# A two-block kernel on one core: the order of transposes, filling products and low parts in the second block's attention

## The chip, the cores and the metric

One core of a Trainium2 chip runs the whole program. The metric is device time in microseconds, the median of several runs. Work goes to in-order queues: TensorE (PE, with its weight loads as PEld), VectorE (DVE), ScalarE (ACT), GpSimd (POOL), and SyncE (SP), which issues most loads.

## The reference, cut to what matters

Two transformer blocks over 256 rows of 1024 columns, in fp32. The first holds two attentions and a mixture of 64 experts. The second holds a mixer and, in its second layer, the attention that the change touches: 16 query heads of 64 columns, 4 key heads, 256 context keys and a window over 256 latent keys, a sink logit for each head.

```
def window_attention(q, k, v, k_ctx, v_ctx, sink):
    ...
        s_win = jnp.einsum('bqkgd,bjkd->bkgqj', qb, kb).astype(jnp.float32) * scale
        s_win = jnp.where(valid, s_win, NEG_INF)
        s_ctx = jnp.einsum('bqkgd,bjkd->bkgqj', qb, k_ctx).astype(jnp.float32) * scale
        p = sink_softmax(jnp.concatenate([s_ctx, s_win], axis=-1), sink_b)
        vals = jnp.concatenate([v_ctx, vb], axis=1)
        return jnp.einsum('bkgqj,bjkd->bqkgd', p.astype(v.dtype), vals)
...
            q, k, v, g = split_c(h @ w_in)
            o = window_attention(q, k, v, k_c, v_c, sink_logit[i])
            y = (o * jax.nn.silu(g)) @ w_out_c[i]
            x = x + gate * y
    return rms_norm_2(x, final_g)
```

## The kernel before, in words

Each engine runs its instructions in the order in which the program emits them. Large products are made from high and low parts: a weight tile is cast to a rounded type on ScalarE (line 129, the high part), VectorE subtracts that from the original (line 130, the low part), and three matmuls (high x high and the two mixed ones) stand in for a product of full precision. Both parts of one unit lie in a tile `hl`, of which there are three.

The class `Dense` holds a queue of such products. Each of its entries has a `prep` (a load of 1 MB for every second unit, then cast and low part, through `hl_unit`) and a `run` (the matmuls, and after the last of a block its evacuation). `step()` fills the queue up to two entries ahead, takes the first, fills again, and runs the entry it took. So a unit is prepared two steps before its products.

The second block's attention is a loop of 19 turns. In turn `n`:

- `w_a(n)`: scores of two heads for one of two query halves into two PSUM banks (two bf16 matmuls add the mask); VectorE takes their maxima (line 2018), joins the sink (2021, 2023); ScalarE takes exponentials with their sums (2027, 2028)
- `w_b(n-1)`: VectorE adds and inverts the sums and scales one head's weights (2033 to 2035), ScalarE the other's (2036)
- `w_d((n-6)/2)`, in even turns from 6 on: weighted sums over values (`ps_o`), gated by VectorE (2061) and split into `hab`, the left operand of the last products (cast 129 on ScalarE, 130 on VectorE)
- `D.step(steps[n])`: the products that fill TensorE: the second half of the queries (turns 0, 1, 3, 4; the rotary position code is applied at turn 4's end, lines 1910 to 1914), the gates (`ps_dt`, with tanh and a product at lines 1932 and 1933 after every second unit), and from turn 13 on the output projection
- `heads(n-2)`, in turns 6 to 9: transposes of two more heads' queries, evacuated by ScalarE and VectorE (1992, 1993)
- `w_t(n-3)`: eight transposes of the weights of turn n-3 into two PSUM banks of a pool of two (`ps_pt`, line 2046), copied out by ScalarE (2051) and VectorE (2049) for `w_d`

`steps` is written out by hand: 2, 1, 0, 1, 1, 1, 0, 0, 2, 1, 1, 0, 1, 1, 0, 1, 0, 1, 0. After the loop come `w_d(7)`, the last products, their residual and the final norm.

Of the kernel before, what the change touches and what calls it, by code (L numbers as in the profile page):

```python
# [10 lines left out]
F = mybir.dt.float32  # L11
# [4 lines left out]
OP = mybir.AluOpType  # L16
# [16 lines left out]
def kernel(ctx: ExitStack, tc: tile.TileContext, A, out, dbg=None):  # L33
    nc = tc.nc
    V, S, G, T = nc.vector, nc.scalar, nc.gpsimd, nc.tensor
# [15 lines left out]
    def bank(shape, name="ps", pool=None):  # L51
        n = 1
        for s in shape[1:]:
            n *= s
        t = (pool or psum).tile([128, 512], F, name=name, tag="ps")
        v = t[:shape[0], :n]
        if len(shape) == 3:
            v = v.rearrange("p (a b) -> p a b", b=shape[2])
        elif len(shape) == 4:
            v = v.rearrange("p (a b c) -> p a b c", b=shape[2], c=shape[3])  # L60
        return v

    def mm(o, l, r, start, stop):
        T.matmul(o, l, r, start=start, stop=stop)  # L64

    def mm3(o, l, r, start, stop):
        mm(o, l[0], r[0], start, False)
        mm(o, l[0], r[1], False, False)
        mm(o, l[1], r[0], False, stop)

    def kp(w2):
        return w2.rearrange("(k p) n -> p k n", p=128)
# [13 lines left out]
    def hl_tile():  # L86
        line.append(line.pop(0))
        return hlp[line[-1]].tile([128, 2, 1024], R, name="hl", tag="hl")

    def load(view, dims):  # L90
        t = raw_tile()
        n = 1
        for d in dims:
            n *= d
        v = t[:, :n]
        if len(dims) == 2:
            v = v.rearrange("p (k n) -> p k n", n=dims[1])
        nc.sync.dma_start(v, view)
        return v
# [28 lines left out]
    def split(hi, lo, src):  # L128
        S.copy(hi, src)  # L129
        V.tensor_tensor(lo, src, hi.bitcast(F), OP.subtract)  # L130

    def hl_unit(raw, pool=None):

        k, n = raw.shape[1], raw.shape[2]
        t = (pool.tile([128, 2, 1024], R, name="hl", tag="hl") if pool else hl_tile())[:, :, :k * n].rearrange("p h (k n) -> p h k n", n=n)
        split(t[:, 0], t[:, 1], raw)
        return t[:, 0], t[:, 1]


# [4 lines left out]
    class Dense:  # L144


        def __init__(self, bufs=3, ahead=2):
            self.bufs, self.ahead, self.live = bufs, ahead, 0
            self.todo, self.ready = [], []

        def nat(self, act, w3, c0, w, evac, plan=None):
            nk = w3.shape[1]
            plan = plan or PLAIN[:nk // 2]
            job = {}

            def prep(q):
                u, s = q // 2, q % 2
                if s == 0:
                    job["raw"] = load(w3[:, 4 * u:4 * u + 4, c0:c0 + w], (4, w))
                job[q] = hl_unit(job["raw"][:, 2 * s:2 * s + 2])  # L160

            def run(parts):
                if "ps" not in job:
                    job["ps"] = [bank([128, 512], "ps_d") for _ in range(2)]
                done = []
                for q, t in parts:
                    hl = job[q]
                    for k in range(2):
                        kk = 2 * q + k
                        mm3(job["ps"][t][:, :w], [a[:, kk, 128 * t:128 * t + 128] for a in act],  # L170
                            (hl[0][:, k], hl[1][:, k]), kk == 0, kk == nk - 1)
                    if q == nk // 2 - 1:
                        done.append(t)
                    if (q, t) == max((x for st in plan for x in st if x[0] == q), key=lambda x: order_of[x]):
                        self.live -= 1
                        del job[q]
                for t in done:
                    evac(t, c0, w, job["ps"][t][:, :w])

            order_of = {x: i for i, x in enumerate(x for st in plan for x in st)}  # L180
            seen = set()
            for parts in plan:
                new = [q for q, _ in parts if q not in seen]
                seen.update(new)
                q = new[0] if new else None
                self.todo.append((q is not None and (lambda q=q: prep(q)), lambda parts=parts: run(parts)))

        def tr(self, act, w3, c0, evac):
            job = {}

            def prep(cb):
                if cb == 0:
                    job["raw"] = load(w3[:, :, c0:c0 + 256], (8, 256))
                job[cb] = hl_unit(job["raw"][:, :, 128 * cb:128 * cb + 128])

            def run(cb):
                if cb == 0:
                    job["ps"] = bank([128, 2, 256], "ps_dt")
                hl = job.pop(cb)
                self.live -= 1  # L200
                for k in range(8):
                    mm3(job["ps"][:, cb], (hl[0][:, k], hl[1][:, k]), (act[0][:, k], act[1][:, k]), k == 0, k == 7)
                if cb == 1:
                    evac(c0, job["ps"])

            for cb in range(2):
                self.todo.append((lambda cb=cb: prep(cb), lambda cb=cb: run(cb)))
# [12 lines left out]
        def step(self, n=1):  # L220
            for _ in range(n):
                self.fill(self.ahead)
                if not self.ready:
                    return
                run = self.ready.pop(0)
                self.fill(self.ahead)
                run()

# [303 lines left out]
    def mixer(D, hook, pool, wk, hT, head):  # L532
# [57 lines left out]
        vg = pool.tile([128, 4], F, name="vg")  # L590
        nc.gpsimd.dma_start(vg, A["v_norm_g_2"].rearrange("o (h c) -> c (o h)", c=128))
        step(4)
        V.tensor_scalar(st_v[:, 0, 0:2], st_v[:, 0, 0:2], 1.0 / 512, None, op0=OP.mult)
        for t in range(2):
# [54 lines left out]
    def residual(wk, x, gate, then=None):  # L649

        def f(t, c0, w, ps):
            tmp = wk.tile([128, 512], F, name="tmp")
            V.tensor_tensor(tmp, ps, gate[:, c0:c0 + w], OP.mult)
            V.tensor_tensor(x[:, t, c0:c0 + w], x[:, t, c0:c0 + w], tmp, OP.add)
            if then:
                then(t)
        return f
# [5 lines left out]
    D = Dense()  # L663
# [558 lines left out]
    D = Dense()  # L1222
# [613 lines left out]
    D, hook, hT = Dense(), {}, []  # L1836
# [24 lines left out]
    with ExitStack() as st:  # L1861
# [4 lines left out]
        with ExitStack() as s2:  # L1866
# [31 lines left out]
            later = gate_later(mx, gb)  # L1898
            D, mx2 = mixer(D, hook, mx, wk, hT, head)
# [131 lines left out]
        def w_b(n):  # L2031
            p, sm, es = wst[n]
            V.tensor_add(sm, sm, es)
            V.reciprocal(sm, sm)
            V.tensor_scalar(p[:, 0], p[:, 0], sm[:, 0:1], None, op0=OP.mult)
            S.activation(p[:, 1], p[:, 1], AF.Copy, scale=sm[:, 1:2])

        def w_t(n):
            c, t = wunits[n]
            p = wst.pop(n)[0]  # L2040
            if t == 0:
                wpt[c] = ring.tile([128, 2048], F, name="w", tag="w").rearrange("p (j k n) -> p j k n", j=2, k=4)
            for j in range(2):
                ps = bank([128, 4, 128], "ps_pt", psbg)
                for kt in range(4):
                    T.transpose(ps[:, kt], p[:, j, 128 * kt:128 * kt + 128], ident)
                o = wpt[c][:, j, :, 128 * t:128 * t + 128]
                if j:
                    V.tensor_copy(o, ps)
                else:  # L2050
                    S.copy(o, ps)

        def w_d(c):
            ps = bank([128, 256], "ps_o")
            pt = wpt.pop(c)
            g = 64 * (c // 2)
            for kt in range(4):
                for j in range(2):
                    mm(ps[64 * j:64 * j + 64], vcat[:, kt, g:g + 64], pt[:, j, kt], kt == 0, kt == 3)
            t1 = wk.tile([128, 256], F, name="t1")  # L2060
            V.scalar_tensor_tensor(t1, ps, 0.5, sg[:, c], op0=OP.mult, op1=OP.mult)
            split(oT[0][:, c], oT[1][:, c], t1)
# [13 lines left out]
        steps = (2, 1, 0, 1, 1, 1, 0, 0, 2, 1, 1, 0, 1, 1, 0, 1, 0, 1, 0)  # L2076
        w_oc = kp(A["w_out_c_2"][0])
        D.nat(oT, w_oc, 0, 512, residual(wk, X, gb))
        for n in range(19):
            if n < 16:  # L2080
                w_a(n)
            if 1 <= n < 17:
                w_b(n - 1)
            if n >= 6 and n % 2 == 0:
                w_d((n - 6) // 2)
            D.step(steps[n])
            if 6 <= n < 10:
                heads(n - 2)
            if 3 <= n:
                w_t(n - 3)  # L2090
        w_d(7)
        fg = load(A["final_g_2"].rearrange("(o d) -> o d", o=1).to_broadcast([128, 1024]), (1024,))
        o = ring.tile([128, 2048], F, name="w", tag="w").rearrange("p (t n) -> p t n", t=2)
# [97 lines left out]
```

## Time and profile before

| | |
|---|---|
| median of 3 runs | 1149.74 us (1148.93 to 1151.8) |
| profiled execution | 1148.99 us |
| its span, first to last instruction | 1146.6 us |
| mean granted TensorE clock | 0.964 |
| busy: TensorE, VectorE, ScalarE | 1041.8 (91%), 668.2 (58%), 401.2 (35%) us |
| moved by DMA | 340.09 MB, 297 GB/s on average |

The span is what the trace covers; the profiled execution's own time is 2.39 us longer. Busy times are sums over the whole program, whose stages have different limits. A busy TensorE is not one at its peak, since matmuls overlap and their ends are modelled: starts are the better measure.

### The profile page before, as it was taken

What the parts mean: (1) busy time and instruction counts of PE and PEld (TensorE: products, weight loads), DVE (VectorE), ACT (ScalarE), POOL (GpSimd) and SP (SyncE); (2) the same over time, 40 slices, a digit from 0 to 9 for tenths busy, and PEclk for the clock granted to TensorE, in tenths of its full rate; (3) what the DMA queues carried; (4) which work ended last, traced back from release to release, by engine and by line L of the source; (5) the groups of instructions that cost most, each with busy time, mean ns of one, the idle gap of its engine ahead of it and who ended that gap; (6) DMA issues with size and microseconds to landing.
All of it is one profiled execution on the core that took longest, in us unless ns stands there. A gap on an engine that the chain in (4) does not pass through costs nothing.

```text
span 1146.6 us, 18395 instructions
## 1 busy us (share of the span) xinstructions
PE 1041.8 (91%) x7241; PEld 707.0 (62%) x7241; DVE 668.2 (58%) x1396; ACT 401.2 (35%) x746; POOL 38.9 (3%) x80
## 2 busy tenths in 40 slices
PE   5899999997899999999988999897988998997886
PEld 1666558776855666565555656564546896765664
DVE  1767666856664454454534555456547677767766
ACT  1453654434133222112121222122315445555653
POOL 2400000000010000000000000000002000000000
PEclk9899899999999999999988999998999999998998
DMA  9977799766648999999998999999959763211110
GB/s 344 394 267 280 273 367 376 278 267 245 252 163 342 414 420 417 419 412 413 412 412 347 384 417 416 416 417 421 420 192 370 246 203 132 74 37 58 37 73 37
DMA packets 86223, 340.09 MB, mean 297 GB/s; under 512 B 6362, under 2 KB 24084, under 8 KB 56432
## 3 DMA queue, kind: packets, MB, share of 16 engines
q1 hardware_dynamic: 82240, 328.74, 73.3%
q0 software_dynamic: 2560, 7.64, 2.0%
q10 hardware_dynamic: 1328, 2.45, 0.6%
q8 instruction: 58, 0.95, 0.3%
q14 instruction: 37, 0.30, 0.1%
HBM read 337.75 MB, written 1.06 MB: 295 GB/s over the span
## 4 chain that ended last, share of the span: by engine, by line
PE 57%; DVE 13%; DMA 11%; ACT 7%; issue 2%; ACTq 0%; SPq 0%; DVEq 0%
PE ps_gu L64 13%; PE ps_d L64 12%; PE ps_dn L64 7%; DMA w<-in_w_exp_down 5%; PE ps_g L64 4%; PE ps_b L64 4%; PE ps_sc L64 3%; DVE hl L130 3%; PE ps_bt L64 3%; PE ps_dt L64 2%; PE ps_ada L64 2%; ACT hl L129 2%; ACT p L2027 2%; DVE nm L2018 1%; PE ps_s L64 1%
## 5 line engine op out<-in xcount | busy, mean ns | idle before, releaser
L130 DVE TENSOR_TENSOR hl<-w,hl 128x1024 fp32r<-128x1024 f32 (+1 forms) x130 | 157.4, 1218 | 88.6 <-ACT hl L129 88.1
L64 PE MATMUL ps_gu<-w,xt 128*32 128x256 f32 (+1 forms) x1824 | 175.3, 396 | 8.0 <-DMA w<-in_w_exp_up 5.2
L129 ACT CAST hl<-w 128x1024 fp32r<-128x1024 f32 (+1 forms) x130 | 134.6, 1042 | 100.6 <-PE ps_d L64 57.4
L64 PE MATMUL ps_d<-hl,hab 128*128 128x512 f32 (+1 forms) x576 | 142.4, 403 | 4.5 <-ACT hl L129 2.2
L64 PEld LDWEIGHTS ps_gu<-w,xt 128*32 128x32 f32 (+1 forms) x1824 | 95.7, 124 | 71.8 <-issue 18.7
L64 PEld LDWEIGHTS ps_d<-hl,hab 128*128 128x128 f32 x576 | 109.3, 193 | 36.0 <-issue 4.1
L129 ACT CAST y<-ys 128x512 fp32r<-128x512 f32 x50 | 30.9, 619 | 242.9 <-DVE ys L1470 242.9
L64 PE MATMUL ps_dn<-w,aT 128*32 128x512 f32 (+1 forms) x456 | 98.5, 601 | 5.0 <-DMA w<-in_w_exp_down 4.4
L1480 DVE TENSOR_TENSOR X<-X,ps_sc 128x512 f32<-128x512 f32 x100 | 64.0, 682 | 44.7 <-PE ps_sc L64 44.7
L64 PE MATMUL ps_b<-hl,hab 128*128 128x512 f32 x240 | 62.3, 409 | 5.4 <-ACT hab L129 2.6
L1470 DVE TENSOR_TENSOR ys<-ps_dn,g 128x512 f32<-128x512 f32 x50 | 34.4, 689 | 52.4 <-PE ps_dn L64 52.1
L64 PE MATMUL ps_dt<-hmh,hl 128*128 128x256 f32 x320 | 60.2, 284 | 0.5 <-ACT p L2027 0.5
L64 PEld LDWEIGHTS ps_b<-hl,hab 128*128 128x128 f32 x240 | 44.6, 192 | 21.1 <-issue 4.9
L130 DVE TENSOR_TENSOR y<-ys,y 128x512 fp32r<-128x512 f32 x50 | 34.6, 693 | 36.2 <-ACT y L129 36.2
L64 PE MATMUL ps_d<-hl,hmh 128*128 128x512 f32 x160 | 51.5, 402 | 3.9 <-DVE hmh L284 3.0
L1454 DVE SCALAR_TENSOR_TENSOR a<-a,gsl,ps_gu 128x256 f32<-128x256 f32 x25 | 12.0, 480 | 73.4 <-PE ps_gu L64 73.4
L64 PE MATMUL ps_g<-sl,xg 128*128 128x256 f32 (+1 forms) x416 | 52.7, 285 | 0.0
L64 PEld LDWEIGHTS ps_dt<-hmh,hl 128*128 128x128 f32 x320 | 49.9, 188 | 1.8 <-issue 0.8
L64 PEld LDWEIGHTS ps_g<-sl,xg 128*128 128x128 f32 x416 | 50.5, 192 | 0.2 <-DVE sl L1379 0.2
L64 PE MATMUL ps_gu<-acc,xt 128*32 128x256 f32 (+1 forms) x224 | 48.6, 405 | 1.9 <-DMA acc<-in_w_exp_up 1.9
L64 PEld LDWEIGHTS ps_dn<-w,aT 128*32 128x32 f32 (+1 forms) x456 | 22.9, 120 | 42.6 <-issue 29.2
L64 PE MATMUL ps_gu<-hl,xt 128*32 128x256 f32 (+1 forms) x192 | 47.6, 404 | 1.7 <-DMA hl<-in_w_exp_up 1.7
(557 smaller groups left out, 1713.6 us busy)
## 6 DMA issues: line engine op xcount, KB each, us to landing
w<-in_w_exp_gate SPq DMA_DIRECT2D x52, 1024.0 KB, 11.2
w<-in_w_exp_down SPq DMA_DIRECT2D x49, 1024.0 KB, 13.5
w<-in_w_exp_up SPq DMA_DIRECT2D x48, 1024.0 KB, 14.7
w<-in_w_ada SPq DMA_DIRECT2D x24, 1024.0 KB, 9.7
w<-in_ada_w SPq DMA_DIRECT2D x24, 1024.0 KB, 8.9
w<-in_w_in_ab SPq DMA_DIRECT2D x18, 1024.0 KB, 11.7
w<-in_w_in SPq DMA_DIRECT2D x14, 1024.0 KB, 12.3
w<-in_w_in_c SPq DMA_DIRECT2D x12, 1024.0 KB, 5.6
```

The costliest lines, as they stand in the source:

```text
L64: T.matmul(o, l, r, start=start, stop=stop)
L129: S.copy(hi, src)
L130: V.tensor_tensor(lo, src, hi.bitcast(F), OP.subtract)
L1454: V.scalar_tensor_tensor(a, a, g["gsl"], ps, op0=OP.mult, op1=OP.mult)
L1470: V.tensor_tensor(ys, ps, g2[:, 512 * n:512 * n + 512], OP.mult)
L1480: V.tensor_add(o, o, ps)
L2018: V.tensor_reduce(nm[:, j:j + 1], ps, AX, OP.max, negate=True)
L2027: S.activation(p[:, j], pss[j], AF.Exp, bias=nm[:, j:j + 1], accum_out=sm[:, j:j + 1])
```

## The change

In a turn, `w_t` (transposes and copies) moves ahead of `D.step` and `heads`. A list, `D.later`, is set for the time of the loop: while it is, `hl_unit` emits the cast at once but puts the low part's instruction on the list, and `lows()` emits what is on it. That happens in each turn after `w_a` and `w_b` and ahead of `w_d`; inside `step` ahead of the second filling and the products, if something is on the list; and once after the loop.

```
-    def hl_unit(raw, pool=None):
+    def hl_unit(raw, pool=None, later=None):
...
-        split(t[:, 0], t[:, 1], raw)
+        if later is None:
+            split(t[:, 0], t[:, 1], raw)
+        else:
+            S.copy(t[:, 0], raw)
+            later.append(lambda: V.tensor_tensor(t[:, 1], raw, t[:, 0].bitcast(F), OP.subtract))
         return t[:, 0], t[:, 1]
...
+            self.later = None
+
+        def lows(self):
+            while self.later:
+                self.later.pop(0)()
...
-                job[q] = hl_unit(job["raw"][:, 2 * s:2 * s + 2])
+                job[q] = hl_unit(job["raw"][:, 2 * s:2 * s + 2], None, self.later)
...
-                job[cb] = hl_unit(job["raw"][:, :, 128 * cb:128 * cb + 128])
+                job[cb] = hl_unit(job["raw"][:, :, 128 * cb:128 * cb + 128], None, self.later)
...
                 run = self.ready.pop(0)
+                if self.later:
+                    self.lows()
                 self.fill(self.ahead)
                 run()
...
         D.nat(oT, w_oc, 0, 512, residual(wk, X, gb))
+        D.later = []
         for n in range(19):
             if n < 16:
                 w_a(n)
             if 1 <= n < 17:
                 w_b(n - 1)
+            D.lows()
             if n >= 6 and n % 2 == 0:
                 w_d((n - 6) // 2)
+            if 3 <= n:
+                w_t(n - 3)
             D.step(steps[n])
             if 6 <= n < 10:
                 heads(n - 2)
-            if 3 <= n:
-                w_t(n - 3)
+        D.lows()
+        D.later = None
         w_d(7)
```

## Rows read from the trace of the kernel before

**Rows 1.** Busy time by stretch: turns 0, 2, 4, 5, 7, 11, 14, tail, loop.

```profile
core 0: us, PE busy (x) PEld busy (x) DVE busy (x) ACT busy (x) POOL busy (x), PEclk, DMA share, GB/s
1006.87:1015.12 8.25, 8.25 (x50) 6.70 (x50) 4.49 (x8) 5.19 (x9) 0.00 (x0) 1.00 0.06 15
1020.95:1023.33 2.38, 2.19 (x14) 1.68 (x12) 2.24 (x9) 0.81 (x3) 0.00 (x0) 1.00 0.00 0
1029.78:1040.20 10.42, 4.89 (x34) 4.00 (x34) 7.96 (x18) 4.18 (x9) 0.00 (x0) 0.88 0.31 100
1040.20:1046.65 6.45, 6.31 (x34) 4.32 (x35) 4.07 (x10) 4.19 (x10) 0.00 (x0) 0.67 0.01 3
1052.55:1058.13 5.58, 5.58 (x35) 3.77 (x34) 3.61 (x10) 3.11 (x8) 0.00 (x0) 0.81 0.00 0
1082.11:1085.09 2.98, 2.84 (x9) 1.82 (x9) 2.84 (x9) 1.39 (x5) 0.00 (x0) 0.50 0.02 5
1098.90:1103.91 5.01, 4.34 (x25) 3.19 (x24) 3.60 (x12) 2.93 (x8) 0.00 (x0) 1.00 0.00 0
1103.91:1118.63 14.72, 11.98 (x82) 8.24 (x80) 7.85 (x20) 6.66 (x14) 0.00 (x0) 1.00 0.01 1
1006.87:1118.63 111.76, 95.11 (x602) 71.60 (x601) 75.70 (x171) 63.35 (x143) 0.00 (x0) 0.94 0.16 53
```

**Rows 2.** Order of time, VectorE, turns 4 and 5: start, duration, instruction, idle before.

```profile
1035.63 0.75 DVE L1910 TENSOR_TENSOR tmp<-ps_d,rt 128x256 f32<-128x256 f32 x2
...
1039.60 0.68 DVE L2049 COPY w<-ps_pt 128x512 f32<-128x512 f32 x1
1040.20 1.28 DVE L2018 TENSOR_REDUCE nm<-ps_s 128x1 f32<-128x512 f32 x2
...
1044.91 1.23 DVE L130 TENSOR_TENSOR hl<-w,hl 128x1024 fp32r<-128x1024 f32 x1 [2.24 <-ACT hl L129]
1046.05 0.68 DVE L2049 COPY w<-ps_pt 128x512 f32<-128x512 f32 x1
```

**Rows 3.** Order of time, ScalarE, turn 5.

```profile
1041.79 0.69 ACT L2027 ACTIVATE p<-ps_s,nm 128x512 f32<-128x512 f32 x1 [0.97 <-DVE nm L2021]
...
1043.22 0.71 ACT L2036 ACTIVATE p<-p,sm 128x512 f32<-128x512 f32 x1
1043.84 1.04 ACT L129 CAST hl<-w 128x1024 fp32r<-128x1024 f32 x1
1044.77 0.59 ACT L2051 COPY w<-ps_pt 128x512 f32<-128x512 f32 x1
```

**Rows 4.** Who waited for whom from 1004 to 1122: total, times, longest.

```profile
DVE hl L130 <- ACT hl L129: 21.0, 11, 3.7
...
PE ps_pt L2046 <- DVE w L2049: 7.2, 4, 5.0
...
PE ps_pt L2046 <- ACT w L2051: 6.7, 4, 3.1
```

**Rows 5.** Order of time, TensorE, turn 10 and the scores of turn 11.

```profile
1070.84 1.95 PE L64 MATMUL ps_o<-w,vcat 128*64 128x256 f32 x16
1072.71 0.39 PE L64 MATMUL ps_dt<-hmh,hl 128*128 128x256 f32 x1
...
1075.65 1.04 PE L2046 MATMUL ps_pt<-cst,p 128*128 128x128 f32 x8
1076.44 0.48 PE L64 MATMUL ps_s<-kkh,hab 128*128 128x512 f32 x1
...
1077.04 0.48 PE L64 MATMUL ps_s<-kkh,hab 128*128 128x512 f32 x1
```

**Rows 6.** Order of time, VectorE, the output's low part in turns 14 and 16.

```profile
1102.96 0.43 DVE L130 TENSOR_TENSOR hab<-t,hab 128x256 fp32r<-128x256 f32 x1 [1.27 <-ACT hab L129]
...
1112.03 0.43 DVE L130 TENSOR_TENSOR hab<-t,hab 128x256 fp32r<-128x256 f32 x1 [0.47 <-ACT hab L129]
```

**Rows 7.** Groups by line and form, VectorE's evacuations from 1000 to 1120.

```profile
L1993 DVE SCALAR_TENSOR_TENSOR hab<-ps_t,hab 64x512 fp32r<-64x512 f32 x6 | 4.2, 694 | 2.9 <-ACT hab L1992 2.8
...
L1933 DVE SCALAR_TENSOR_TENSOR sg<-sg,ps_dt 128x512 f32<-128x512 f32 x4 | 2.7, 680 | 0.0
```

**Rows 8.** Order of time: SP's last issue of weights, and their first cast.

```profile
1091.36 0.37 SPq L98 DMA_DIRECT2D w<-in_w_out_c  x1
...
1121.95 2.00 ACT L129 CAST hl<-w 128x1024 fp32r<-128x1024 f32 x2
```

## The prediction

> **What bounds the kernel now.** I read the page first: TensorE is busy for 91% of the span, but that is an average over stages. The change touches one loop, the nineteen turns of the second block's window attention, so I cut the trace there: from the first maximum (turn 0, at 1006.87) to the last weighted sum over values, `w_d(7)`, at 1118.63 [rows 1]. Those 111.76 us hold 95.11 us of TensorE, 75.70 of VectorE and 63.35 of ScalarE: none is full. So I read VectorE's and ScalarE's instructions in order of time.
>
> Turn 5 shows the pattern [rows 2, 3]. Maximum at 1040.20; ScalarE starts the exponentials at 1041.79 (1.59 later), the scaling of the previous turn's weights at 1043.22 (1.43 on), the cast that makes a high part at 1043.84 (0.62 on), and its transpose copy at 1044.77 (0.93 on). VectorE, idle for 2.24 us, starts the low part at 1044.91, its transpose copy at 1046.05 (1.14 on), and the next maximum at 1046.65 (0.60 on). The period, 6.45 us, is a relay: maximum, exponentials, scaling, cast, low part, copy, maximum. In the loop VectorE waits 21.0 us in eleven such places for the cast of the weights [rows 4]. TensorE also waits, up to 5.0 us at a time, for the copies that empty the two banks of its transposes, but behind those waits stand only the next turn's scores, whose maximum cannot start before that same copy.
>
> What TensorE has to do follows from starts at the full clock [rows 5]: `w_d` 1.87, a unit of products 2.94, eight transposes 0.79, scores 1.20 (twice the 0.60 between the halves). Up to `w_d(7)`: 7 x 1.87 + 14 x 2.94 + 16 x 0.79 + 16 x 1.20, and four half-sized groups of transposes for heads (0.40 each), 87.7 us. A unit of 12 wide matmuls is taken as equal to 24 half as wide. So there is slack for about 20 us, and the limit is VectorE's order.
>
> **What the change does to a turn.** No instruction is added or removed; no DMA is added, and SP's queue keeps its order of loads. Three things move.
>
> Low parts: in turn n VectorE no longer stands behind this turn's cast. It makes the low part prepared in the turn before, after maximum, sums and scaling. Its cast ended about a microsecond before: ScalarE is through with it 1.59 + 1.43 + 0.62 + 0.60 + 0.93 = 5.2 us after that turn's maximum, and VectorE comes to it at 4.1 + 2.4 = 6.5. The products that use it come after that, two steps after the preparation. Only the first of two steps in turns 0 and 8 still has its low part behind its own cast.
>
> Copies: the transposes stand before the products, and their copies before the cast, on ScalarE, and before the evacuations of products, on VectorE. Turn 4 shows what that is worth: there the copy stood behind 3.97 us of rotary work (1035.63 to 1039.60 [rows 2]).
>
> Periods, maximum to maximum, are therefore VectorE's own work. Turn 2 has no step and no copy: 2.38. Turn 11 has a copy and no low part: 2.98. Turn 14, with `w_d` and no low part: 5.01 [rows 1]. To these I add 1.14 for a pending low part; in a turn with `w_d` only 0.35 of it, since most falls into the wait for the output's cast: VectorE waits 1.27 there [rows 6], and 0.47 where the cast has nothing ahead of it, so 0.80 is cover. With that cover gone it would cost all 1.14. Evacuations come on top: 0.68 for a gate, 0.69 for heads [rows 7], and in turns 8, 9 and 12 the wait for ScalarE's copy, cast and tanh (0.48 to 0.93 each) before them, since these now run after the copy.
>
> In this order, turns 0 to 14: 7.6 (gate before the first low part, the second low part moved on; it is 8.25 now), 3.52, 3.52, 2.98, 8.09 (4.12 + 3.97 of rotary work), 4.12, 6.15 (5.37 + heads), 5.5 (as now, 5.58: heads wait for ScalarE), 8.5, 7.05, 5.37, 4.12, 6.63, 4.12, 5.37. Sum 82.6. Now it is 97.04 (1006.87 to 1103.91): 14.4 less by turn 15's maximum. Turns 2 and 11 are longer than now by 1.14 each, turn 6 and turn 14 by some 0.3; filled turns such as 5 (6.45 to 4.12) pay for it.
>
> The tail, from turn 15's maximum to `w_d(7)`, is 14.72 now [rows 1]. By the new order: copy 2.98 after the maximum; in turn 16 the last low part waits for its cast (5.2), 1.14, `w_d(5)`'s product and cast and low part (1.3), copy 0.69, then TensorE alone: transposes 0.9, products 2.94, `w_d(6)` 1.87, transposes, copies, 1.5. Sum 15.1 to 15.5: 0.4 to 0.8 more. Net 14.0 less. What follows `w_d(7)`, 28 us, keeps its order.
>
> Whether TensorE keeps up: a ring is now closed by the two transpose banks. Copy in turn n, transposes in n+1, products, scores, maximum n+2: 4.12 + 0.1 + 0.79 + 2.94 + 0.65 = 8.6 us for two turns, against VectorE's 8.24 for two filled ones without evacuation; with anything else in either turn it does not decide. Bounds: nothing to 0.4 us at each of three places. I take nothing at two and keep 1.2 for the range. The Trainium skill, Perfetto Trace Analysis, Optimization Strategy, says that the same gap repeating on an engine can mean too little SBUF or PSUM for the next tile. By it the wait for two banks would outlast the reordering; the sum would then be the ring's, 1.2 us less gain at most. The trace agrees that copies release TensorE, but they are late in it for VectorE's waits.
>
> Loads: the last two are issued while turn 12 runs (1091.36), 30.6 us before their cast (1121.95) [rows 8]; one waits for a low part that now comes a turn later, about 7 us, the end comes 14 earlier: 9 us or more are left. Nothing taken.
>
> **The sum.** Profiled execution: span 1146.6, time 1148.99; 14.0 less is 1135.0. The median of the runs is 0.75 higher than that execution, so 1135.8. Its own range, from 1133 (ScalarE's waits in turns 7 to 12 shorter than I set them, 3 us) to 1139 (ring 1.2, a few waits of 0.3 to 0.6).
>
> **Rivals.**
>
> *TensorE falls to half its clock on the path* (gain partly lost). For it: the clock granted in turn 5 was 0.67 and in turn 11 0.50, after TensorE had waited 5 and 3 us for copies [rows 1, 4], and eight transposes then took twice as long. Against it: now such work lies behind VectorE anyway; in the new order the longest wait I find is about 2 us. If it strikes four turns where TensorE is close to deciding (12 to 17), at about 2 us for each (the doubling of 0.79 and 1.20), 8 us come back: 1144. Some of it, 1139 to 1144.
>
> *The same, through the whole loop* (slower). Without the first scores the work from 1006.87 on is 86.5 us; at a mean granted clock of 0.75 it takes 115.3, 3.5 more than now's 111.76, and there the sign turns. At 0.67, as in turn 5, it takes 129: 17 slower, 1167. The loop has 0.94 now. The Trainium skill, TensorE: Matmul & The Clock Gate, in its section on cycling through the PSUM queue, tells of such a loop: small idle pieces between groups of matmuls let the clock swing and throughput falls. By that rule the forecast turns round. The trace speaks against it in turn 14: waits and a clock of 1.00.
>
> *The wait only changes its name.* If casts are late on ScalarE, the moved low parts wait again, now ahead of `w_d` and the copies, which wait behind them on VectorE's queue, and TensorE's transposes behind those. Up to 1.14 us would be paid in each of the five turns that had none (2, 6, 11, 14, 16), and of the 21.0 us of waits half would come back: 14.0 - 10.5 = 3.5 less, 1146. Against it: 1.3 us of margin in each turn.
>
> *No gain at the end.* The last weights arrive late because a tile of the ring is released by `w_d(6)` or `w_d(7)` now: up to 3.5 us back, 1139. Against it: the 9 us above.
>
> **Chances.** As worked out 0.72; clock partly lost, or the last weights, 0.14; better than 1133, 0.05; the wait renamed, within 0.3%, 0.05; slower by the clock 0.04. A change of 0.3% (3.4 us) is about what a measurement of this kernel can tell from none. Faster 0.92, same 0.05, slower 0.03 (a little of the last case stays within the bound). The range 1132.5 to 1141.5 takes in the first case and part of the second.
>
> **What the profile after should show.** VectorE's low parts with no wait for casts, except in turns 0, 8 and 16: the 21.0 us fall below 6. Filled turns without `w_d` at 4.1 to 4.5 instead of 6.45, turn 4 near 8, turns 2 and 11 longer by 1.1. The loop at some 98 us, TensorE's wait for transpose banks standing before products. The stretch after `w_d(7)` at 28. Wrong would be: a granted clock below 0.85 in the loop, low parts that still wait for casts, or filled turns near 6, which would mean that I missed a link of the relay.

## The result, and the profile after

| | before | after |
|---|---|---|
| median of 6 runs each | 1151.76 us | 1135.88 us |
| profiled execution | 1148.99 us | 1133.02 us |
| its span | 1146.6 us | 1131.3 us |
| loop, first maximum to `w_d(7)` | 111.76 us | 97.89 us |

The ratio to the kernel before is 0.987, with a 95% interval of 0.9854 to 0.9886: faster. Two later sets of runs of the same kernel gave 0.9866 [0.9847, 0.9885] and 0.9859 [0.9844, 0.9874].

The span is 15.3 us shorter. The loop has 13.87 of that. The stretch behind `w_d(7)` is 28.02 us, as before (1146.6 - 1118.63 = 27.97), and 1.48 lie ahead of the loop, where no instruction changed: the first maximum starts at 1005.39 instead of 1006.87, but in the profiles of further kernels with the same program up to there it starts anywhere from 1003.96 to 1009.04. So the median meets the forecast more closely than the argument could; what it worked out is the loop.

In the kernel after, lines from 132 on have moved by 4 to 11: 139 is the loop's cast of weights and 140 its low part, 2029 the maximum, 2038 the exponentials, 2057 the transposes, 2060 and 2062 their copies. Busy time by stretch, for the same turns as [rows 1] (0, 2, 4, 5, 7, 11, 14, tail, loop):

```profile
core 0: us, PE busy (x) PEld busy (x) DVE busy (x) ACT busy (x) POOL busy (x), PEclk, DMA share, GB/s
1005.39:1012.99 7.60, 7.60 (x46) 5.96 (x45) 3.35 (x6) 5.19 (x9) 0.00 (x0) 1.00 0.01 2
1016.53:1020.06 3.53, 3.53 (x22) 2.52 (x22) 3.39 (x10) 3.07 (x8) 0.00 (x0) 1.00 0.27 90
1023.04:1031.14 8.10, 7.52 (x48) 6.13 (x48) 7.89 (x19) 6.28 (x14) 0.00 (x0) 1.00 0.00 0
1031.14:1035.26 4.12, 4.12 (x35) 2.99 (x33) 3.98 (x11) 3.15 (x9) 0.00 (x0) 1.00 0.01 4
1041.44:1046.92 5.48, 4.57 (x36) 3.07 (x35) 3.63 (x9) 3.12 (x8) 0.00 (x0) 1.00 0.00 0
1068.01:1072.12 4.11, 3.80 (x28) 2.16 (x26) 3.97 (x10) 2.98 (x8) 0.00 (x0) 1.00 0.20 75
1082.85:1088.19 5.34, 3.66 (x28) 2.41 (x24) 4.73 (x12) 4.07 (x10) 0.00 (x0) 1.00 0.64 198
1088.19:1103.28 15.09, 13.42 (x88) 9.42 (x85) 7.96 (x20) 6.56 (x14) 0.00 (x0) 1.00 0.00 1
1005.39:1103.28 97.89, 89.39 (x602) 68.11 (x601) 75.34 (x171) 63.44 (x143) 0.00 (x0) 1.00 0.18 60
```

VectorE's work is the same (75.34 us against 75.70); its idle time in the loop fell from 36.1 to 22.6. In turns 2, 5 and 11 it now hardly pauses. The granted clock is 1.00 in all of these stretches.

Turn 5 in order of time on VectorE, to be held against [rows 2]:

```profile
1031.14 1.28 DVE L2029 TENSOR_REDUCE nm<-ps_s 128x1 f32<-128x512 f32 x2
...
1033.52 1.22 DVE L140 TENSOR_TENSOR hl<-w,hl 128x1024 fp32r<-128x1024 f32 x1
1034.66 0.68 DVE L2060 COPY w<-ps_pt 128x512 f32<-128x512 f32 x1
1035.26 1.28 DVE L2029 TENSOR_REDUCE nm<-ps_s 128x1 f32<-128x512 f32 x2
```

The low part starts 2.38 us after the maximum, with no idle time before it, where it started 4.71 after with 2.24 idle. ScalarE's side of the same turn [rows 3]:

```profile
1032.73 0.69 ACT L2038 ACTIVATE p<-ps_s,nm 128x512 f32<-128x512 f32 x1 [0.85 <-DVE nm L2032]
...
1034.16 0.72 ACT L2047 ACTIVATE p<-p,sm 128x512 f32<-128x512 f32 x1
1034.78 0.58 ACT L2062 COPY w<-ps_pt 128x512 f32<-128x512 f32 x1
1035.24 1.06 ACT L139 CAST hl<-w 128x1024 fp32r<-128x1024 f32 x1
```

The cast starts at 1035.24, when VectorE is about to take the next maximum: it is out of the relay. ScalarE still waits for the maximum, 0.85 us where it was 0.97. The waits that answer to [rows 4]:

```profile
DVE sg L1944 <- ACT sg L1943: 7.5, 4, 4.2
...
PE ps_pt L2057 <- ACT w L2062: 6.9, 6, 1.7
...
DVE hl L140 <- ACT hl L139: 1.1, 1, 1.1
```

Of 21.0 us of waits for casts in eleven places, 1.1 us in one (turn 16) is left. Not all of that was saved: VectorE now waits 7.5 us for the tanh of the gates, which on ScalarE stands behind the cast (turns 0, 8, 9 and 12; 4.2 of it in turn 0), where it had waited for none [rows 7]. TensorE waits for its transpose banks six times, 1.7 us at most.

### The profile page after: what moved, and what is told of

Same layout as the page of the kernel before. It is cut to its first block, busy times and chain, and to the rows that moved or that the text cites. A ratio compares the mean times of both kernels' runs of the same rounds, so it can differ in the third digit from the quotient of the medians.

```text
span 1131.3 us, 18396 instructions
## 1 busy us (share of the span) xinstructions
PE 1035.2 (92%) x7241; PEld 702.3 (62%) x7241; DVE 668.0 (59%) x1396; ACT 401.3 (35%) x746; POOL 39.0 (3%) x80
## 4 chain that ended last, share of the span: by engine, by line
PE 63%; DVE 14%; DMA 14%; ACT 6%; issue 2%; ACTq 0%; SPq 0%; DVEq 0%
PE ps_d L64 15%; PE ps_gu L64 13%; PE ps_dn L64 6%; DMA w<-in_w_exp_down 5%; PE ps_g L64 4%; PE ps_b L64 4%; PE ps_sc L64 3%; PE ps_bt L64 3%; DMA w<-in_w_exp_up 3%; PE ps_ada L64 3%; PE ps_dt L64 2%; DVE hl L130 2%; PE ps_s L64 2%; DMA w<-in_w_ada 2%; DVE nm L2029 2%
## 5 line engine op out<-in xcount | busy, mean ns | idle before, releaser
L130 DVE TENSOR_TENSOR hl<-w,hl 128x1024 fp32r<-128x1024 f32 (+1 forms) x117 | 141.6, 1218 | 67.0 <-ACT hl L129 66.5
L129 ACT CAST hl<-w 128x1024 fp32r<-128x1024 f32 (+1 forms) x117 | 121.1, 1042 | 99.9 <-PE ps_d L64 56.7
L64 PEld LDWEIGHTS ps_d<-hl,hab 128*128 128x128 f32 x576 | 108.1, 191 | 36.1 <-DVE hl L130 4.2
```

## The experiments

All were timed in five rounds against the kernel before. Edits are to the changed kernel.

**First: low parts alone.** The transposes go back behind products and heads.

```
-            if 3 <= n:
-                w_t(n - 3)
             D.step(steps[n])
             if 6 <= n < 10:
                 heads(n - 2)
+            if 3 <= n:
+                w_t(n - 3)
```

> Low parts deferred, transposes and copies left behind products and heads. Theory (VectorE's wait for the cast was the link that mattered): most of the 15 us stays, ratio to before 0.989 to 0.992, that is 9 to 13 us faster; the loop from first maximum to w_d(7) takes 99 to 103 us; lost against the full change are the copies' 0.6 us that no longer lie in the waits for gates and heads in turns 7, 8, 9 and 12. Rival (the order of transposes and products made the gain): less than half of it, ratio above 0.994.

Measured: 1134.47 us, ratio 0.9866 [0.9846, 0.9886]: all of the gain, more than I expected. Turn 4, tail and loop by stretch:

```profile
1024.77:1032.87 8.10, 7.84 (x52) 6.50 (x50) 7.89 (x19) 6.28 (x14) 0.00 (x0) 1.00 0.00 0
1090.42:1103.75 13.33, 11.57 (x81) 7.94 (x79) 7.94 (x20) 6.56 (x14) 0.00 (x0) 1.00 0.00 1
1007.12:1103.75 96.63, 89.94 (x602) 68.38 (x601) 75.31 (x171) 63.44 (x143) 0.00 (x0) 1.00 0.18 61
```

The loop is 1.26 us shorter than with both parts. From the first to the sixteenth maximum it takes 83.30 us against 82.80: the transposes' move saves 0.5 in all, about 0.1 in each of turns 7, 8, 9 and 12, where I had expected 0.6. The tail gives back 1.76. The rival falls: the transposes' place made no gain.

**Second: transposes alone.** Without the list, each low part stands behind its own cast again.

```
-        D.later = []
```

> Transposes and copies first, low parts left behind their own cast. Theory: the relay maximum, exponentials, scaling, cast, low part, maximum is still closed; a filled turn takes 1.59 + 1.43 + 0.62 + 0.48 + 0.95 + 0.12 + 1.14 = 6.3 us instead of 6.45, and the whole is 0 to 2 us faster, ratio 0.998 to 1.000. Rival (order made the gain): 7 us or more, ratio below 0.994.

Measured: 1149.12 us, ratio 0.999 [0.9975, 1.0004], no change. Turns 4 and 5, tail and loop, then the waits:

```profile
1028.91:1039.23 10.32, 9.38 (x60) 7.46 (x61) 7.98 (x18) 4.19 (x9) 0.00 (x0) 0.94 0.28 80
1039.23:1045.57 6.34, 4.17 (x28) 3.09 (x24) 4.07 (x10) 4.19 (x9) 0.00 (x0) 0.86 0.10 37
1102.15:1118.02 15.87, 14.88 (x87) 10.79 (x86) 7.86 (x20) 6.66 (x14) 0.00 (x0) 0.90 0.00 1
1006.12:1118.02 111.90, 96.59 (x601) 73.67 (x600) 75.75 (x171) 63.35 (x143) 0.00 (x0) 0.92 0.16 52
```

```profile
DVE hl L130 <- ACT hl L129: 19.9, 11, 3.7
```

The relay is closed as before: a filled turn takes 6.34 us (worked out: 6.3), and the eleven waits are back.

**Third: more work for TensorE.** One more matmul ahead of each head's scores, overwritten by them.

```
                 ps = bank([128, 512], "ps_s")
+                mm(ps, qS[:, 2 * c + j, 128 * t:128 * t + 128], kk[0][:, c // 2], True, True)
```

> The full change, and one more matmul of 128 by 512 columns ahead of each head's scores, overwritten by them: 32 in all at 0.24 to 0.32 us, 7.7 to 10 us more for TensorE in the loop. Theory (VectorE's order sets the period, TensorE has some 10 us to spare): at most 2 us slower than the full change, loop 98 to 100 us. Rival (TensorE sets the loop now): all of it, loop 105 to 108 us.

Measured: 1136.97 us, ratio 0.9888 [0.9868, 0.9908]; loop 99.05 us, 1.16 longer, with 6.4 us more of TensorE busy (95.76 against 89.39). Five sixths of the work vanish in its waits. What does not vanish lies in turns 0 to 4, 0.20 to 0.25 us in each: there VectorE comes to wait for the scores (0.18 us ahead of turn 2's maximum). From turn 5 on every turn keeps its length within 0.02: there TensorE does not set the loop.

**Fourth: each low part twice.**

```
             later.append(lambda: V.tensor_tensor(t[:, 1], raw, t[:, 0].bitcast(F), OP.subtract))
+            later.append(lambda: V.tensor_tensor(t[:, 1], raw, t[:, 0].bitcast(F), OP.subtract))
```

> The full change, each of the loop's 13 low parts made twice, 1.14 us of VectorE each. Theory (the period is the sum of VectorE's own work): every one of them lengthens the loop, by 1.14 each less what little cover is left: 12 to 15 us, loop 110 to 113 us, which takes the whole gain back; a filled turn takes 5.26 instead of 4.12. Rival (TensorE or ScalarE sets the loop now): less than 6 us.

Measured: 1150.33 us, ratio 1.0001 [0.9988, 1.0015]; loop 113.44, 15.55 longer for 13 more instructions of 1.2 us. Each of the eleven turns that hold one is longer by its full price, 1.24 to 1.27; the tail is longer by 1.71 for its two, at a granted clock of 0.84 there. Turn 5 on VectorE:

```profile
1038.89 1.22 DVE L140 TENSOR_TENSOR hl<-w,hl 128x1024 fp32r<-128x1024 f32 x1
1040.14 1.23 DVE L141 TENSOR_TENSOR hl<-w,hl 128x1024 fp32r<-128x1024 f32 x1
1041.29 0.68 DVE L2061 COPY w<-ps_pt 128x512 f32<-128x512 f32 x1
```

The second starts 1.25 us after the first, and everything behind it slides; there is no cover to speak of. This and the run before it name the bound: VectorE's own sequence, with the waits that stand in it.

**Fifth: the tail.** From turn 15 on, products stand before the transposes, and the loop's last cast comes later.

```
-            if 3 <= n:
-                w_t(n - 3)
-            D.step(steps[n])
+            if n < 15:
+                if 3 <= n:
+                    w_t(n - 3)
+                D.step(steps[n])
+            else:
+                if steps[n]:
+                    D.ready.pop(0)()
+                w_t(n - 3)
+                if n == 16:
+                    D.fill(2)
+                    D.lows()
```

> The full change up to turn 14; from turn 15 on products stand ahead of the transposes again, and the last cast and low part of the loop follow turn 16's copies. Theory (in the last turns TensorE is the limit, and the new order makes it wait 1.68 us in turn 15 and 1.25 in turn 17 for the copies, with the products behind): the stretch from turn 15's maximum to w_d(7) falls from 15.1 to about 12.6 us, the loop from 97.9 to about 95.4, some 2.5 us faster than the full change. Rival (the tail is paced by VectorE's and ScalarE's chain of sums, cast and copy as the turns are): within 0.5 us of the full change.

Measured: 1133.47 us, ratio 0.9847 [0.9822, 0.9871], not told apart from the full change by time. By its trace the tail takes 11.90 us instead of 15.09, the loop 94.70. TensorE in the tail of the full change, and then of this run:

```profile
1087.76 1.23 PE L2057 MATMUL ps_pt<-cst,p 128*128 128x128 f32 x8 [1.68 <-ACT w L2062]
1088.74 3.03 PE L64 MATMUL ps_d<-hl,hab 128*128 128x512 f32 x12
...
1095.92 1.23 PE L2057 MATMUL ps_pt<-cst,p 128*128 128x128 f32 x8 [1.25 <-ACT w L2062]
1096.91 3.04 PE L64 MATMUL ps_d<-hl,hab 128*128 128x512 f32 x12
```

```profile
1089.52 3.04 PE L64 MATMUL ps_d<-hl,hab 128*128 128x512 f32 x12
1092.40 1.03 PE L2057 MATMUL ps_pt<-cst,p 128*128 128x128 f32 x8
```

With products first, they start behind the scores and the copy is done when the transposes come: the 1.68 us are gone. The run changes two things at once, but the first run has the order alone: its tail is 13.33. So of the 3.2 us, 1.76 belong to the order and 1.43 to the cast's place. In the first run the cast stands ahead of a copy on ScalarE, and half of turn 17's transposes wait for that copy; here the wait is nearly gone:

```profile
1095.63 0.65 PE L2057 MATMUL ps_pt<-cst,p 128*128 128x128 f32 x4 [1.14 <-ACT w L2062]
```

```profile
1096.10 0.66 PE L2057 MATMUL ps_pt<-cst,p 128*128 128x128 f32 x4 [0.20 <-ACT w L2062]
```

**Sixth: low parts on GpSimd.**

```
-            later.append(lambda: V.tensor_tensor(t[:, 1], raw, t[:, 0].bitcast(F), OP.subtract))
+            later.append(lambda: G.tensor_tensor(t[:, 1], raw, t[:, 0].bitcast(F), OP.subtract))
```

> The full change with the loop's 13 low parts made by GpSimd, which is idle there. Theory (VectorE's own work sets the period): a filled turn falls towards TensorE's 4.9 us or stays at 4.1, turn 11 goes to 2.98 and turns 6, 10, 14 to 5.01 plus heads; the loop 90 to 95 us if GpSimd needs less than 5 us for one. From the rows of before (128 by 32 in 0.49 us, 128 by 128 in 1.0) I estimate 5 to 6 us for 128 by 1024; then the two units of turns 0, 1 and 8, 9 come late, TensorE waits for low parts, and the loop is 95 to 103 us. Rival (VectorE does not set it): no gain even where the low part is in time.

Measured: 1135.6 us, ratio 0.9871 [0.9852, 0.9889]; loop 97.94, no gain. My price was wrong: GpSimd needs 2.4 us for one, so the low parts are not late by their own length. Turn 5 does fall to 2.98 and turn 10 to 5.02, as the theory wants. But turn 11 takes 4.44, and the order of time shows why:

```profile
1069.85 1.28 DVE L2029 TENSOR_REDUCE nm<-ps_s 128x1 f32<-128x512 f32 x2
...
1070.39 2.38 POOL L140 TENSOR_TENSOR hl<-w,hl 128x1024 fp32r<-128x1024 f32 x1 [5.07 <-ACT hl L139]
...
1071.16 1.62 DVE L2032 SCALAR_TENSOR_TENSOR nm<-sk,nm 128x2 f32<-128x2 f32 x1
```

VectorE's product of two columns, 0.16 us elsewhere, takes 1.62 and ends when GpSimd's subtraction does (1070.39 + 2.38 = 1072.77). The maximum, whose input lies in PSUM, runs beside it undisturbed. The held product stands in the relay, so the exponentials are late by 1.46, more than the 1.14 that was saved. VectorE is busy for 69.96 us, though 13 instructions of 1.22 (15.9) left its 75.34: so 10.5 us are put down to such holds. The Trainium skill, SBUF — State Buffer, section on its two separate sides, tells of a read and write port pair that VectorE and GpSimd share and that an instruction holds to its end against VectorE's instructions with two inputs in SBUF. The trace agrees: 1.62 us for an instruction of 0.16.

**Seventh: low parts behind `w_d`'s output.**

```
-            D.lows()
+            if n == 16:
+                D.lows()
             if n >= 6 and n % 2 == 0:
                 w_d((n - 6) // 2)
+            D.lows()
```

> The full change, with the low parts behind w_d's output on VectorE instead of ahead of it (turn 16 left as it is). Theory (0.8 of a low part's 1.14 us lies in VectorE's wait for the output's cast): turns 6, 10 and 14 take 6.95, 6.15 and 6.15 us instead of 6.18, 5.36 and 5.34; the loop is 2.4 us longer, 100.3. Rival (order within VectorE's turn does not matter, only which turn): no difference.

Measured: 1138.34 us, ratio 0.9897 [0.988, 0.9914]; loop 100.27. Turns 6, 10 and 14 take 6.99, 6.15 and 6.15, every other turn what it took. The cover of 0.8 us is real, and it is lost if the low part does not stand where VectorE would wait.

**Eighth and eleventh: the full change again**, to stand beside the runs on their chips.

> The full change as it is, on the same chip as the three others, to compare them with: ratio to before 0.985 to 0.989, loop 97.9 us.

> The full change on the same chip as the twelfth run: ratio to before 0.985 to 0.989.

Measured: 1134.38 and 1134.53 us, the ratios given above; in the eighth, loop 97.88 us and every turn within 0.02 of the first profile.

**Ninth: the waits that are left.** On top of the fifth run, the pending low part goes inside `w_d`, and the turn's cast behind the evacuations.

```
-            split(oT[0][:, c], oT[1][:, c], t1)
+            S.copy(oT[0][:, c], t1)
+            D.lows()
+            V.tensor_tensor(oT[1][:, c], t1, oT[0][:, c].bitcast(F), OP.subtract)
...
-            D.lows()
             if n >= 6 and n % 2 == 0:
                 w_d((n - 6) // 2)
+            else:
+                D.lows()
...
-            D.step(steps[n])
+            for i in range(steps[n]):
+                if i:
+                    D.fill(2)
+                    D.lows()
+                D.ready.pop(0)()
             if 6 <= n < 10:
                 heads(n - 2)
...
+            if n == 16 or steps[n] and n != 15:
+                D.fill(2)
...
```

> The fifth run's tail; in turns with w_d the pending low part stands between the gated product and the output's low part, inside VectorE's wait for the output's cast; and the turn's cast of weights comes last on ScalarE, behind the tanh of a gate and the heads. Theory (VectorE's work and the waits left on its queue set the turns): turns 6, 10, 14 lose 0.35 us each (10 and 14 take 5.0), turn 0 0.65, turn 8 0.6, turns 9 and 12 0.9 each; the loop from first maximum to w_d(7) takes 91 to 92 us against 94.7, some 6 faster than the full change. Rival (TensorE is now the limit): the loop stays within 1 us of 94.7.

Measured: 1130.18 us, ratio 0.9838 [0.982, 0.9857]; loop 91.70:

```profile
1004.81:1096.51 91.70, 88.08 (x602) 68.11 (x601) 75.58 (x171) 63.16 (x143) 0.00 (x0) 1.00 0.20 64
```

Turns 6, 8, 9, 10, 12 and 14 take 5.85, 7.98, 6.20, 5.03, 5.66 and 5.01 us. Against the full change, 3.95 us are gained by turn 15's maximum; the tail is 12.85, 0.95 longer than in the fifth run, for a cause that was not sought. The tanh no longer stands behind the cast, and VectorE's waits for it fall from 7.5 us in four places to 3.8 in two (3.2 of it in turn 0, where the tanh stands behind the exponentials):

```profile
DVE sg L1944 <- ACT sg L1943: 3.8, 2, 3.2
```

TensorE is now busy for 88.08 of 91.70, and the prediction counts 86.5 that it has to do from the first maximum on, so an estimate of what is left to gain in the loop is some 5 us.

**Tenth and twelfth: the same, products ahead of the transposes in all turns.**

> The same as the ninth run, but products and heads ahead of the transposes in every turn, as in the kernel before. Theory (the transposes' place was worth nothing by itself): the loop is within 1.5 us of the ninth run's, longer by up to 0.6 in turns 8, 9 and 12, where the copies no longer lie in waits. Rival (with the waits gone the transposes' place now matters): 3 us or more longer.

> The tenth run's kernel on the same chip as the full change. If the loop's 6 us reach the time, it is 5 to 7 us faster than the full change, ratio to before 0.980 to 0.984, and its interval lies apart from the other's. Rival (what the loop gives is lost outside it): within 2 us of the full change.

Measured: in the tenth, 1128.64 us, ratio 0.9827 [0.9807, 0.9848] and a loop of 91.75 us, the ninth's within 0.05 (0.58 longer by turn 15's maximum, 0.53 shorter behind it); in the twelfth, 1127.78 us, ratio 0.9809 [0.9793, 0.9825], beside the full change's 0.9859 [0.9844, 0.9874] on the same chip. The intervals lie apart: this version is 6.7 us faster than the full change and beats both kernels, without the transposes' move.

## Why the prediction was right

**The bound.** Shown: the loop follows VectorE's sequence. Twice the low parts took the whole gain back (fourth run); more work for TensorE cost a sixth of itself, all of it in turns 0 to 4 (third).

**The periods.** The fifteen turns were worked out at 82.6 us and measured at 82.80; the largest misses are turns 8 and 9 (8.5 and 7.05 against 8.59 and 7.14). For these two and turn 12 the prediction gives its waits only as a band, 0.48 to 0.93 us each, so their closeness says less than that of the others. Turns 2 and 11 did get longer, by 1.15 and 1.13, and turn 14 by 0.33. The term of 0.35 for a low part in a turn with `w_d` came out at 5.34 - 5.01 = 0.33 and was tested by itself (seventh run).

**The tail.** 15.09 us, forecast 15.1 to 15.5, and by the path that was worked out: turn 16's low part starts 5.20 us after turn 15's maximum, behind a wait for its cast. The prediction counted it as a price of the change; the first and fifth runs show that it is one of the order there and of the cast's place, and avoidable.

**The transposes' place.** Here the prediction was wrong, and the time does not show it. It offered turn 4 as what the copies' move is worth, because the copy stood behind 3.97 us of rotary work. But that work fills VectorE before the next maximum on either side of the copy: turn 4 takes 8.10 us with the move and without it (first run), 10.32 with the move alone (second). What I had written as two parts of one gain was one part. The move's own worth is half a microsecond in waits for ScalarE, less 1.76 in the tail.

**The rivals.** The clock did not fall: 1.00 in every stretch of the loop, where it had been 0.94 over all of it, with TensorE's waits for its banks at 1.7 us at most instead of 5.0. Both clock rivals fall. The Trainium skill's section on cycling through the PSUM queue (TensorE: Matmul & The Clock Gate) does not describe the changed loop: the short waits are there, the swings are not. Why the clock stays up is not shown: in the second run no wait of the matmuls is longer than 1.86 us either, and its loop has 0.92. Nor did the filled turns gain by the clock. Before the change, turns 3 and 13 took the same 6.45 us at 1.00 as turn 5 at 0.67:

```profile
1023.33:1029.78 6.45, 4.99 (x22) 3.31 (x22) 4.06 (x11) 4.90 (x12) 0.00 (x0) 1.00 0.00 1
1092.45:1098.90 6.45, 6.45 (x42) 4.56 (x40) 4.07 (x10) 3.57 (x8) 0.00 (x0) 1.00 0.44 163
```

The low parts wait for a cast again in turn 16 alone (1.1 us), not in turns 0 and 8 as well, as the prediction had it. But the wait for ScalarE did change its name in part: the 7.5 us for the tanh. The prediction has these within its periods of turns 0, 8, 9 and 12, not as a rival, and the ninth run shows that they were avoidable in part. The last weights are issued at 1082.40, 24.2 us before their cast at 1106.60, so the late load did not come. The ring of transpose banks was not tried by itself; no turn is longer for it.

**What the total owes to chance.** The argument gave 14.0 us for the loop, and 13.87 came. The medians moved by 15.9: executions of one kernel lie up to 4.4 us apart (1133.02 to 1137.4), and the trace of the profiled one is 1.48 us shorter ahead of the loop.

## What to carry to other kernels

Where two engines hand work to and fro, find the instruction that waits for a result of its own turn although that result is needed a turn or two later, and put it a turn behind: it then costs its length and not the relay's. Count what the new order does by the sequence of the engine that sets the period, turn by turn; a part of a change that moves work on an engine with slack may be worth next to nothing (0.5 us here). Put deferred work where the bounding engine would wait anyway, and treat the last turns, where the limit is another, by themselves.

## What the runs showed of the hardware

GpSimd subtracts 128 x 1024 in 2.4 us, twice VectorE's 1.22 and not the five that I had put together from smaller rows. While it did, instructions of VectorE with inputs in SBUF stood still: one of two columns (0.16 us became 1.62), and the scaling of weights by a column of factors in turn 14 (0.49 became 2.37), while a maximum over PSUM ran on. Over thirteen such subtractions VectorE lost 10.5 us: idle GpSimd was no free helper here.
